# A two-layer trunk on one core: the causal mask of layer 1 as a VectorE addition in PSUM, the head's loads on two queues, and SP's loads in the order of the code

## The chip, the cores and the metric

The kernel runs on one core of one Trainium2 chip. The metric is device time in microseconds (us), the median of three executions; beside them one execution was profiled. The core's engines each work through a queue of their own, in order: TensorE (PE, with its weight loads as PEld), VectorE (DVE), ScalarE (ACT), GpSimd (POOL) and SyncE (SP), which only starts transfers here. ACT can start transfers too. Matmul results stand in PSUM, all else in SBUF.

## The reference

Two layers, each `x <- LayerNorm(ALPHA * x + mixer(x))`, on 256 tokens of 1024 values with 16 heads of 64. Layer 0 selects 64 keys for each query by an index score and runs softmax attention over them; layer 1 is stick-breaking attention, which the mask belongs to.

```python
def dsa_mixer(x, w_in, w_out, cos, sin):            # layer 0
    q, k, v, g, qi, wi, ki = split(x @ w_in)        # q, k, qi, ki get rope
    score = einsum('bqhs,bqh->bqs', relu(qi . ki * 64 ** -0.5), wi)
    _, idx = top_k(where(key_chunk <= q_chunk, score, -inf), 64)
    p = softmax(q . k[idx] * 64 ** -0.5)
    return (p @ v[idx] * silu(g)) @ w_out

def stick_breaking_mixer(x, w_in, w_out):           # layer 1
    q, k, v, g = split(x @ w_in, 4)
    z = einsum('bqhd,bshd->bhqs', q, k) * 64 ** -0.5
    before = pos[None, :] < pos[:, None]            # key strictly earlier than query
    log_one_minus = where(before, log_sigmoid(-z), 0.0)
    log_stick = cumsum(log_one_minus, axis=3, reverse=True) - log_one_minus
    a = where(before, exp(log_sigmoid(z) + log_stick), 0.0)
    return (a @ v * silu(g)) @ w_out
```

## The kernel before, in words

Numbers are kept to 32-bit accuracy by splitting each operand into a high part (written by ACT as a copy to `fp32r`) and a low part (DVE: source minus high), and by three matmuls for each product. `split` (L65 to L67) does it: `wh`, `wl` are the parts of a chunk of weights, `xT` those of the transposed input, `sh`, `sl` those of the stick logits.

**Weights.** They stream as 80 chunks of 128x1024 (512 KB) over SP's queue. `fetch` (L79) starts the load of a chunk into one of four `raw` buffers and splits it; `load_chunk` keeps two chunks ahead (`AHEAD`). A load can start only when its `raw` buffer has been split.

**Head.** `WARM` matmuls on zeros (L167) run on PE first. Eight loads `x_idx` (L172 to L179) bring, for each of the eight slices k of the model dimension, 256 columns of transposed x and 584 columns of index weights; the first slice comes in two loads, one on SP and one on ACT. Behind them come the first chunk, the constants `cs` (identity, triangle, causal mask, rope tables), and a copy `cr` of three of them by POOL. The index projections are the matmuls of L228; `rope` (L211 to L218, tiles `ra` and `rb`) rotates them, and PE transposes them to `qih`, `qil` (L249, L250) and `zh`, `zl` (padded keys).

**Layer 0.** `mix` runs the projections of half of q, k and v (`tok_part`, L113) turn by turn with `select` (index scores L136, top-64). Then a loop over pairs of heads runs key transposes, logits, softmax and values of successive pairs in one iteration, with the other projections, the gates (L145) and the output projection in between. At its fifth step (`s == 4`) the program text has the two loads of `x` and the two of `gb` (layer-norm scale and shift, 128x1024 each). `out_norm` is the output projection with the residual and layer norm.

**Layer 1.** Values and gates first, with the loads of layer 1's `gb` ahead of them. Then one loop over pairs j, with the stages of different pairs in one iteration: `queries1` (L158 is the copy `low`, L159 adds it in PSUM, `zh`/`zl` are the padded queries), `values1` every second pair, `keys1` (`kh`, `kl`), `logits1` of the pair before and `sticks1` of the one before that. `logits1` writes, for each of two key tiles t, three matmuls (L573 is the last) and the mask (L576) into a PSUM bank; then ACT takes abs, exp and ln (`ab`, L579 to L581), DVE max/add (L582), and the result is split to `sh`, `sl`. `sticks1` adds the triangle products of them (L595 to L597) into the same banks, and ACT takes the exponential `aw` (L602).

**Order.** A tile scheduler sets the order of each engine's queue before the run, by its own estimates and not strictly by the program text; `keep_in_program_order` pins an instruction to its place in the text. So a load can stand in SP's queue far ahead of where the text has it, or behind it.

Of the kernel before, what the change touches and what calls it, by code (L numbers as in the profile page):

```python
# [10 lines left out]
F32R = mybir.dt.float32r  # L11
AF = mybir.ActivationFunctionType
OP = mybir.AluOpType

P = 128
S = 256
D = 1024
KT = D // P
NT = S // P
# [13 lines left out]
IDX_W = IH * HD + HD + IH  # L33
# [4 lines left out]
C_ID, C_TRI, C_CAUS, C_ADM0, C_ADM1, C_COS, C_SIN = 0, 128, 256, 384, 512, 768, 896  # L38
# [4 lines left out]
def trunk(ctx: ExitStack, tc: tile.TileContext, x_rows, x_idx, w_all, consts, lnp, out):  # L43
    nc = tc.nc

    def pool(name, bufs, **kw):
        return ctx.enter_context(tc.tile_pool(name=name, bufs=bufs, **kw))
# [4 lines left out]
    cst = pool("cst", 1)  # L52
# [7 lines left out]
    def as32(t):  # L60
        return t.bitcast(F32)
# [1 line left out]
    nc.scalar.preload_act_table_set("exp_and_others")  # L63

    def split(h, lo, src):  # L65
        nc.scalar.activation(h, src, AF.Copy)  # L66
        nc.vector.tensor_sub(lo, src, as32(h))  # L67


    def feature_major(name):  # L70
        a = sb.tile([P, KT, 2, S], F32R, name=name, tag="aT")
        return a, a[:, :, 0], a[:, :, 1]

    _, xTh, xTl = feature_major("xT")

    ahead = []
    n_chunk = [0]

    def fetch():  # L79
        c = n_chunk[0]  # L80
        if c == w_all.shape[0]:
            return
        n_chunk[0] += 1
        raw = wraw.tile([P, CW], F32, name="raw", tag="raw")
        nc.sync.dma_start(raw, w_all[c])
        wh = wspl.tile([P, CW], F32R, name="wh", tag="wh")
        wl = wspl.tile([P, CW], F32R, name="wl", tag="wl")
        split(wh, wl, raw)
        ahead.append((wh, wl))
# [9 lines left out]
    def bank(p, w=512):  # L99
        return p.tile([P, 512], F32, name="bank", tag="bank")[:, :w]  # L100
# [15 lines left out]
    def tok_block(src):  # L116

        ps = [bank(pp) for _ in range(NT)]
        for c, wc in enumerate(load_block()):
            if c:  # L120
                yield
            tok_part(list(enumerate(ps)), src, wc, c)
        return ps

    def mix(*gens):

        live = list(gens)
        while live:
            for g in list(live):
                try:  # L130
                    next(g)
                except StopIteration:
                    live.remove(g)
# [36 lines left out]
    cuts = (slice(0, IDX_A), slice(IDX_A, IDX_W))  # L170
    idx_w = []
    for k in range(KT):  # L172
        raw = wraw.tile([P, CW], F32, name="raw", tag="raw")[:, :S + IDX_W]
        if k:
            nc.sync.dma_start(raw, x_idx[k])
        else:
            first = S + IDX_A
            nc.sync.dma_start(raw[:, :first], x_idx[k, :, :first])
            nc.scalar.dma_start(raw[:, first:], x_idx[k, :, first:])  # L179
        wh = wspl.tile([P, CW], F32R, name="wh", tag="wh")[:, :IDX_W]  # L180
        wl = wspl.tile([P, CW], F32R, name="wl", tag="wl")[:, :IDX_W]
        split(xTh[:, k], xTl[:, k], raw[:, :S])
        for c in cuts[:1 + (k == 0)] if k == 0 else (slice(0, IDX_W),):
            split(wh[:, c], wl[:, c], raw[:, S + c.start:S + c.stop])
        idx_w.append((wh, wl))

    fetch()
    cs = cst.tile([P, C_W], F32, name="cs")
    nc.sync.dma_start(cs, consts)
    ident = cs[:, C_ID:C_ID + P]  # L190
    adm = [cs[:, C_ADM0:C_ADM0 + P], cs[:, C_ADM1:C_ADM1 + S]]
    cos = cs[:, C_COS:C_COS + P].rearrange("p (t d) -> p t d", t=2)
    sin = cs[:, C_SIN:C_SIN + P].rearrange("p (t d) -> p t d", t=2)
    cr = cst.tile([P, 3, P], F32R, name="cr")
    nc.gpsimd.tensor_copy(cr, cs[:, :3 * P].rearrange("p (a b) -> p a b", a=3))
    identr, trir, causr = cr[:, 0, :], cr[:, 1, :], cr[:, 2, :]
    onesr = cst.tile([P, P], F32R, name="onesr")
    neg1 = cst.tile([P, P], F32, name="neg1")
    nc.gpsimd.memset(neg1, -1.0)
# [22 lines left out]
    for k in range(KT):  # L222
        w = idx_w[k]
        for xp, wp in ((0, 0), (1, 0), (0, 1)):
            xk = (xTh, xTl)[xp]
            for t in range(NT):
                for n in range(2):
                    nc.tensor.matmul(psi[t][n][:, :cuts[n].stop - cuts[n].start],  # L228
                                     xk[:, k, t * P:(t + 1) * P], w[wp][:, cuts[n]],
                                     start=k + xp + wp == 0, stop=k == 7 and wp == 1)  # L230
    for _ in range(AHEAD):
        fetch()
# [14 lines left out]
    def feat_split(h, lo, src, scale=None):  # L247
        if scale is None:
            nc.scalar.activation(h, src, AF.Copy)  # L249
            nc.vector.tensor_sub(lo, src, as32(h))  # L250
        else:
            nc.scalar.activation(h, src, AF.Copy, scale=scale)
            nc.vector.scalar_tensor_tensor(lo, src, scale, as32(h), op0=OP.mult, op1=OP.subtract)
# [15 lines left out]
    for j in range(2):  # L269
# [5 lines left out]
        pv = pt.rearrange("p (a s) -> p a s", a=2)  # L275
# [38 lines left out]
    def q_block(half):  # L314
        ps = yield from tok_block(xs)
        rr = []
        for t in range(NT):
            r = wk.tile([P, 8, HD], F32, name=f"rq{t}", tag=f"s{t}")
            rope(r, ps[t], 8, t)
            rr.append(r)  # L320
        for j in range(2):
            pt = bank(at)
            for a in range(2):
                for t in range(NT):
                    nc.tensor.transpose(pt[:, (2 * a + t) * P:(2 * a + t + 1) * P],
                                        rr[t][:, 4 * j + 2 * a:4 * j + 2 * a + 2, :], ident)
            for a in range(2):
                g = 4 * half + 2 * j + a
                feat_split(qh[g], ql[g], pt[:, a * S:(a + 1) * S], -SCALE)
        yield  # L330

    def k_block(half):
        ps = yield from tok_block(xs)
        for t in range(NT):
            rope(kr[t][:, 8 * half:8 * half + 8], ps[t], 8, t)
        yield
# [18 lines left out]
    def v_block(n):  # L355
        tiles = yield from tok_block(xs)
        for t, ps in enumerate(tiles):
            keep_v(ps, n, t)
        yield
# [92 lines left out]
    g_b = {}  # L452
# [44 lines left out]
    def load_gb(layer):  # L497
        for i in range(2):
            g_b[layer, i] = cst.tile([P, D], F32, name=f"gb{layer}{i}", tag=f"gb{i}")
            nc.sync.dma_start(g_b[layer, i], lnp[2 * layer + i:2 * layer + i + 1, :].to_broadcast([P, D]))  # L500

    def chain(*gens):
        for g in gens:
            yield from g

    def gates(src):
        for j in range(NPAIR):
            gate(j, src)
            yield

    x = [sb.tile([P, D], F32, name=f"x{t}", tag=f"x{t}") for t in range(NT)]
# [10 lines left out]

    mix(chain(q_block(0), k_block(0), v_block(0)), select())
    fill = chain(k_block(1), q_block(1), v_block(1), gates(xs), out_norm(0, x, turn))
    for s in range(NPAIR + 3):
        if s == 4:
            for t in range(NT):
                nc.sync.dma_start(x[t], x_rows[t * P:(t + 1) * P, :])
            load_gb(0)
        for c in "kfvFlft":  # L530
            if c == "f" or (c == "F" and s < 4):
                next(fill, None)
            elif c != "F":
                d, stage = {"k": (0, keys0), "l": (1, logits0), "t": (2, turn0), "v": (3, values0)}[c]
                if 0 <= s - d < NPAIR:
                    stage(s - d)
    for _ in fill:
        pass
    load_gb(1)


    ys = [(yTh[:, k], yTl[:, k]) for k in range(KT)]
# [21 lines left out]
    def logits1(j):  # L564
        z = zpad[j % 2]
        kh, kl = held.pop(j)
        pz, sp = [], []
        for t in range(NT):
            n = (NT - t) * P
            ks = slice(t * P, (t + 1) * P)  # L570
            pv = bank(at, 2 * n).rearrange("p (a q) -> p a q", a=2)
            qs = slice(t * P, S)
            nc.tensor.matmul(pv, kh[:, ks], z[0][:, :, qs], start=True, stop=False)  # L573
            nc.tensor.matmul(pv, kh[:, ks], z[1][:, :, qs], start=False, stop=False)
            nc.tensor.matmul(pv, kl[:, ks], z[0][:, :, qs], start=False, stop=False)
            nc.tensor.matmul(pv[:, :, :P], identr, causr[:, None, :].to_broadcast([P, 2, P]),  # L576
                             start=False, stop=True)
            a = wk.tile([P, 2, n], F32, name=f"ab{t}", tag=f"b{n}")
            nc.scalar.activation(a, pv, AF.Abs)  # L579
            nc.scalar.activation(a, a, AF.Exp, scale=-1.0)  # L580
            nc.scalar.activation(a, a, AF.Ln, bias=1.0)  # L581
            nc.vector.scalar_tensor_tensor(a, pv, 0.0, a, op0=OP.max, op1=OP.add)  # L582
            sh = wk.tile([P, 2, n], F32R, name=f"sh{t}", tag=("s0", "pT0")[t])
            sl = wk.tile([P, 2, n], F32R, name=f"sl{t}", tag=("s1", "pT1")[t])
            split(sh, sl, a)
            pz.append(pv)
            sp.append((sh, sl))
        held[j] = pz, sp
# [19 lines left out]
            weighted_v(*((jj, lambda i, aw=held[jj]: aw[0][:, i, :], lambda i, aw=held[jj]: aw[1][:, i, :])  # L608
                         for jj in (j - 1, j)))

    for _ in gates(ys):
        pass
    tc.keep_in_program_order(nc.scalar.preload_act_table_set("natural_log_exp_and_others"))
    def store(t, n):
        ns = slice(n * 512, (n + 1) * 512)
# [92 lines left out]
```

## Time and profile before

| | us |
|---|---|
| three runs, median | 315.13 |
| the three runs | 314.31, 315.13, 315.16 |
| profiled execution, its own time | 313.89 |
| its span in the trace | 312.1 |
| PE busy | 299.8 (96%) |
| DVE busy | 246.3 (79%) |
| ACT busy | 191.7 (61%) |
| POOL busy | 7.7 (2%) |

The profiled execution is one more run with its own time; the span is what its trace covers, and 1.79 us lie around it. Busy shares are means over the whole span: stages with different limits lie behind them.

### The profile page before, as it was taken

Reading aid. Unit: us, or ns where it says so; the run is one execution under the profiler, and the core shown is the slowest. Engines: PE = TensorE matmul, PEld = TensorE weight load, DVE = VectorE, ACT = ScalarE, POOL = GpSimd, SP = SyncE. Lnnn points to the kernel's source line nnn. Section 1 sums busy time; section 2 is a strip of 40 time slices with the busy share of each in tenths; the row PEclk is TensorE's granted clock in tenths of the full one; section 3 lists DMA queues with packets and bytes.
Section 4 is the critical chain, followed back from the end, with each engine's and each line's share of the span. In section 5 each row is a group of like instructions: output and inputs, shape, how many; then the busy total and the mean of one; then the engine's idle time right before and its main releaser. Section 6 shows DMA issues by size and latency. Waiting matters only on the chain.

```text
span 312.1 us, 4825 instructions
## 1 busy us (share of the span) xinstructions
PE 299.8 (96%) x1722; PEld 256.3 (82%) x1722; DVE 246.3 (79%) x538; ACT 191.7 (61%) x388; POOL 7.7 (2%) x16
## 2 busy tenths in 40 slices
PE   8998799998999999999999999999999999999990
PEld 5986688886888899988888888888888888887790
DVE  3777989998999999997589576776788887872375
ACT  5655445385346998875415377657799998975200
POOL 3010000000000000000010100000000000000011
PEclk9999799999999999999999999999999999999997
DMA  7898736586044846574424858866553253000003
GB/s 255 270 328 284 274 111 202 186 280 209 4 131 137 268 138 187 186 234 140 133 67 127 275 161 295 287 197 198 167 163 100 69 159 100 2 0 2 0 13 121
DMA packets 14423, 50.40 MB, mean 161 GB/s; under 512 B 1600, under 2 KB 1728, under 8 KB 14400
## 3 DMA queue, kind: packets, MB, share of 16 engines
q1 hardware_dynamic: 14256, 49.97, 49.3%
q8 instruction: 13, 0.21, 0.3%
q10 hardware_dynamic: 144, 0.14, 0.1%
q14 instruction: 10, 0.08, 0.1%
HBM read 49.05 MB, written 1.05 MB: 161 GB/s over the span
## 4 chain that ended last, share of the span: by engine, by line
PE 78%; DVE 10%; DMA 6%; issue 3%; ACT 2%; DVEq 0%; SPq 0%; ACTq 0%
PE bank L113 32%; PE bank L153 14%; PE bank L145 7%; PE bank L155 7%; DMA raw<-w_all 4%; DVE wl L67 4%; PE bank L368 3%; DMA raw<-x_idx 2%; PE bank L596 1%; PE bank L136 1%; PE bank L369 1%; DVE sc L293 1%; ACT wh L66 1%; DVE sc L300 1%; PE bank L138 1%
## 5 line engine op out<-in xcount | busy, mean ns | idle before, releaser
L67 DVE TENSOR_TENSOR wl<-raw,wh 128x1024 fp32r<-128x1024 f32 (+2 forms) x89 | 103.5, 1165 | 23.1 <-ACT wh L66 22.4
L66 ACT ACTIVATE wh<-raw 128x1024 fp32r<-128x1024 f32 (+2 forms) x89 | 90.0, 1016 | 50.2 <-DMA raw<-w_all 25.6
L113 PE MATMUL bank<-wh,xT 128*128 128x512 f32 x192 | 50.8, 400 | 1.2 <-DVE rb L216 1.2
L153 PE MATMUL bank<-yT,wh 128*128 128x512 f32 x192 | 48.3, 394 | 0.0
L113 PEld LDWEIGHTS bank<-wh,xT 128*128 128x128 f32 x192 | 35.9, 191 | 8.7 <-issue 1.6
L153 PEld LDWEIGHTS bank<-yT,wh 128*128 128x128 f32 x192 | 34.5, 189 | 6.9 <-issue 0.3
L155 PEld LDWEIGHTS bank<-yT,wl 128*128 128x128 f32 x192 | 26.2, 190 | 1.9
L113 PE MATMUL bank<-wl,xT 128*128 128x512 f32 x96 | 27.6, 396 | 0.0
L155 PE MATMUL bank<-yT,wl 128*128 128x256 f32 x192 | 26.8, 282 | 0.0
L113 PEld LDWEIGHTS bank<-wl,xT 128*128 128x128 f32 x96 | 18.4, 192 | 3.7
L113 PE MATMUL bank<-wh,ol 128*128 128x512 f32 (+1 forms) x80 | 20.5, 350 | 0.0
L113 PE MATMUL bank<-wh,oh 128*128 128x512 f32 (+1 forms) x80 | 20.4, 354 | 0.0
L113 PE MATMUL bank<-wl,oh 128*128 128x512 f32 (+1 forms) x80 | 20.2, 348 | 0.0
L113 PE MATMUL bank<-wh,yT 128*128 128x512 f32 x64 | 17.4, 391 | 0.0
L145 PE MATMUL bank<-xT,wh 128*128 128x256 f32 x128 | 16.9, 285 | 0.0
L425 ACT ACTIVATE p<-ml,mx 128x128 f32<-128x128 f32 (+1 forms) x32 | 14.3, 447 | 3.7 <-DVE mx L420 3.4
L145 PEld LDWEIGHTS bank<-xT,wh 128*128 128x128 f32 x128 | 16.1, 190 | 0.4
L113 PEld LDWEIGHTS bank<-wh,ol 128*128 128x128 f32 x80 | 14.1, 189 | 2.1 <-issue 0.2
L113 PEld LDWEIGHTS bank<-wl,oh 128*128 128x128 f32 x80 | 14.1, 189 | 1.9
L113 PEld LDWEIGHTS bank<-wh,oh 128*128 128x128 f32 x80 | 13.6, 189 | 2.2 <-issue 0.5
L113 PEld LDWEIGHTS bank<-wh,yT 128*128 128x128 f32 x64 | 12.0, 188 | 2.4
L582 DVE SCALAR_TENSOR_TENSOR ab<-bank,ab 128x512 f32<-128x512 f32 (+1 forms) x16 | 8.5, 555 | 6.3 <-ACT ab L581 5.9
(140 smaller groups left out, 507.3 us busy)
## 6 DMA issues: line engine op xcount, KB each, us to landing
raw<-w_all SPq DMA_DIRECT2D x80, 512.0 KB, 4.3
raw<-x_idx SPq DMA_DIRECT2D x7, 420.0 KB, 4.1
gb<-lnp SPq DMA_DIRECT2D x4, 512.0 KB, 6.9
x<-x_rows SPq DMA_DIRECT2D x2, 512.0 KB, 6.5
y<-x SPq DMA_DIRECT2D x4, 256.0 KB, 2.0
cs<-consts SPq DMA_DIRECT2D x1, 512.0 KB, 6.8
raw<-x_idx SPq DMA_DIRECT2D x1, 288.0 KB, 2.9
raw<-x_idx ACTq DMA_DIRECT2D x1, 132.0 KB, 3.1
```

What stands on the lines that cost most here:

```text
L66: nc.scalar.activation(h, src, AF.Copy)
L67: nc.vector.tensor_sub(lo, src, as32(h))
L113: nc.tensor.matmul(ps, src[kk][xp][:, t * P:(t + 1) * P], wc[wp][:, k, :], start=kk == 0 and xp + wp == 0, stop=kk == 7 and wp == 1)
L136: nc.tensor.matmul(ps, sh, mh, start=first, stop=False)
L138: nc.tensor.matmul(ps, sl, mh, start=False, stop=last)
L145: nc.tensor.matmul(ps, w[wp][:, k, :], src[k][xp], start=k + xp + wp == 0, stop=k == 7 and wp == 1)
L153: nc.tensor.matmul(ps, wh[:, k, :], yT[:, k], start=k == 0, stop=k == 7)
L155: nc.tensor.matmul(ps[:, :S], wl[:, k, :], yTh[:, k], start=False, stop=k == 7, skip_group_check=True)
L293: nc.vector.scalar_tensor_tensor(sc, rel[:, a, :], wi[t][:, h:h + 1], prev, op0=OP.mult, op1=OP.add)
L368: nc.tensor.matmul(po[rs, n * S:(n + 1) * S], vt[0][:, hs], p0(i), start=True, stop=False)
L425: nc.scalar.activation(p[:, i, :], m[:, i, :], AF.Exp, bias=mx[:, c], scale=-1.0, accum_out=sm[:, c])
L582: nc.vector.scalar_tensor_tensor(a, pv, 0.0, a, op0=OP.max, op1=OP.add)
```

## The change

It has three parts. (1) The causal mask of layer 1 is added by DVE to the logits where they stand in PSUM, and no longer by a matmul of the identity with the mask; of the three constants that POOL copied only the triangle is still needed. (2) The first slice of the head comes in three loads (x on SP, 320 columns of weights on ACT, 264 on SP), slices 1 and 3 are loaded by ACT's queue, the x part of the first slice is split by DVE alone, and ACT's two copies for it are pinned in program order. (3) All of SP's loads are pinned in program order, the x rows and layer 0's `gb` come one at each step from the fifth on, and layer 1's `gb` are loaded in its gates, the first behind two of them.

```diff
+    def load(dst, src):
+        tc.keep_in_program_order(nc.sync.dma_start(dst, src))
...
-        nc.sync.dma_start(raw, w_all[c])
+        load(raw, w_all[c])
...
         if k:
-            nc.sync.dma_start(raw, x_idx[k])
+            (nc.scalar.dma_start if k in (1, 3) else load)(raw, x_idx[k])
         else:
             first = S + IDX_A
-            nc.sync.dma_start(raw[:, :first], x_idx[k, :, :first])
-            nc.scalar.dma_start(raw[:, first:], x_idx[k, :, first:])
+            load(raw[:, :S], x_idx[k, :, :S])
+            nc.scalar.dma_start(raw[:, S:first], x_idx[k, :, S:first])
+            load(raw[:, first:], x_idx[k, :, first:])
...
-        split(xTh[:, k], xTl[:, k], raw[:, :S])
...
+        if k:
+            split(xTh[:, k], xTl[:, k], raw[:, :S])
+        else:
+            nc.vector.tensor_copy(xTh[:, k], raw[:, :S])
+            nc.vector.tensor_sub(xTl[:, k], raw[:, :S], as32(xTh[:, k]))
+        for c in cuts if k == 0 else (slice(0, IDX_W),):
+            copy = split(wh[:, c], wl[:, c], raw[:, S + c.start:S + c.stop])
+            if k == 0:
+                tc.keep_in_program_order(copy)
...
-    cr = cst.tile([P, 3, P], F32R, name="cr")
-    nc.gpsimd.tensor_copy(cr, cs[:, :3 * P].rearrange("p (a b) -> p a b", a=3))
-    identr, trir, causr = cr[:, 0, :], cr[:, 1, :], cr[:, 2, :]
+    caus = cs[:, C_CAUS:C_CAUS + P]
+    trir = cst.tile([P, P], F32R, name="trir")
+    nc.gpsimd.tensor_copy(trir, cs[:, C_TRI:C_TRI + P])
...
-            nc.sync.dma_start(g_b[layer, i], lnp[2 * layer + i:2 * layer + i + 1, :].to_broadcast([P, D]))
+            load(g_b[layer, i], lnp[2 * layer + i:2 * layer + i + 1, :].to_broadcast([P, D]))
+            yield
...
+    def rows():
+        for t in range(NT):
+            load(x[t], x_rows[t * P:(t + 1) * P, :])
+            yield
+
+    extra = chain(rows(), load_gb(0))
     for s in range(NPAIR + 3):
-        if s == 4:
-            for t in range(NT):
-                nc.sync.dma_start(x[t], x_rows[t * P:(t + 1) * P, :])
-            load_gb(0)
+        if s >= 4:
+            next(extra, None)
...
-    load_gb(1)
...
-            nc.tensor.matmul(pv, kl[:, ks], z[0][:, :, qs], start=False, stop=False)
-            nc.tensor.matmul(pv[:, :, :P], identr, causr[:, None, :].to_broadcast([P, 2, P]),
-                             start=False, stop=True)
+            nc.tensor.matmul(pv, kl[:, ks], z[0][:, :, qs], start=False, stop=True)
+            nc.vector.tensor_add(pv[:, :, :P], pv[:, :, :P], caus[:, None, :].to_broadcast([P, 2, P]))
...
-    for _ in gates(ys):
-        pass
+    mix(gates(ys), chain((None for _ in range(2)), load_gb(1)))
```

On SP's queue this is the stretch of the kernel before behind the constants, with the loads of weights (`raw`), layer-norm rows (`gb`, named by their number) and x rows:

```order
L85 DMA raw<-w_all 128x1024 x6
L500 DMA gb_1165<-lnp 128x1024
L500 DMA gb_1167<-lnp 128x1024
L85 DMA raw<-w_all 128x1024
L528 DMA x_373<-x_rows 128x1024
L85 DMA raw<-w_all 128x1024 x2
L528 DMA x_374<-x_rows 128x1024
L85 DMA raw<-w_all 128x1024 x42
L500 DMA gb_2015<-lnp 128x1024
L500 DMA gb_2017<-lnp 128x1024
```

And this is the same stretch of the changed kernel:

```order
L79 DMA raw<-w_all 128x1024 x25
L79 DMA x_374<-x_rows 128x1024
L79 DMA raw<-w_all 128x1024 x2
L79 DMA x_375<-x_rows 128x1024
L79 DMA raw<-w_all 128x1024 x2
L79 DMA gb_1424<-lnp 128x1024
L79 DMA raw<-w_all 128x1024 x2
L79 DMA gb_1565<-lnp 128x1024
L79 DMA raw<-w_all 128x1024 x21
L79 DMA gb_2258<-lnp 128x1024
L79 DMA raw<-w_all 128x1024
L79 DMA gb_2290<-lnp 128x1024
```

The four loads that stood behind the sixth to ninth chunk after the constants now stand behind the 25th to 31st, one at a time, and layer 1's two have a chunk between them.

On ACT's queue this is one iteration of layer 1's loop before, for the pair whose stick logits are `ab_3059` and `ab_3073` (pair 5, counted from 0); `aw` are the exponentials of the pair ahead of it, `sh` the high parts:

```order
L579 ACTIVATE ab_3059<-bank 128x512
L579 ACTIVATE ab_3073<-bank 128x256
L580 ACTIVATE ab_3059<-ab_3059 128x512
L580 ACTIVATE ab_3073<-ab_3073 128x256
L249 ACTIVATE kh<-bank 128x256
L581 ACTIVATE ab_3059<-ab_3059 128x512
L581 ACTIVATE ab_3073<-ab_3073 128x256
L602 ACTIVATE aw_3088<-bank 128x512
L602 ACTIVATE aw_3090<-bank 128x256
L66 ACTIVATE sh_3064<-ab_3059 128x512
L66 ACTIVATE sh_3078<-ab_3073 128x256
L158 ACTIVATE low<-bank 128x256
```

And this is the same pair in the changed kernel, where the numbers are one higher:

```order
L617 ACTIVATE aw_3091<-bank 128x256
L617 ACTIVATE aw_3089<-bank 128x512
L261 ACTIVATE kh<-bank 128x256
L594 ACTIVATE ab_3060<-bank 128x512
L594 ACTIVATE ab_3074<-bank 128x256
L595 ACTIVATE ab_3060<-ab_3060 128x512
L595 ACTIVATE ab_3074<-ab_3074 128x256
L596 ACTIVATE ab_3060<-ab_3060 128x512
L596 ACTIVATE ab_3074<-ab_3074 128x256
L163 ACTIVATE low<-bank 128x256
L66 ACTIVATE wh<-raw 128x1024
L66 ACTIVATE sh_3065<-ab_3060 128x512
```

The exponentials `aw` have moved from behind the logarithms to ahead of the abs, and a copy `low` and a weight copy `wh` now stand between the logarithms and `sh`.

On DVE's queue this is the same pair in the changed kernel, from the addition of `low` for its iteration to the low parts `sl`; before, the rows from `kl` on were `kl`, the two max/add, the two `sl`, the addition of `low` and `wl`:

```order
L164 TENSOR_TENSOR bank<-bank,low 128x256
L592 TENSOR_TENSOR bank<-bank,cs 128x2x128
L592 TENSOR_TENSOR bank<-bank,cs 128x256
L67 TENSOR_TENSOR wl<-raw,wh 128x1024
L262 TENSOR_TENSOR kl<-bank,kh 128x256
L597 SCALAR_TENSOR_TENSOR ab_3060<-bank,ab_3060 128x512
L597 SCALAR_TENSOR_TENSOR ab_3074<-bank,ab_3074 128x256
L164 TENSOR_TENSOR bank<-bank,low 128x256
L67 TENSOR_TENSOR wl<-raw,wh 128x1024
L67 TENSOR_TENSOR sl_3066<-ab_3060,sh_3065 128x512
L67 TENSOR_TENSOR sl_3080<-ab_3074,sh_3079 128x256
```

The two masks (L592) are new, one for each key tile, and the addition of the next `low` and a weight split `wl` have moved ahead of `sl`.

## Rows read from the trace of the kernel before

**Rows 1.** The page: span, and busy time of each engine.

```profile
span 312.1 us, 4825 instructions
PE 299.8 (96%) x1722; PEld 256.3 (82%) x1722; DVE 246.3 (79%) x538; ACT 191.7 (61%) x388; POOL 7.7 (2%) x16
```

**Rows 2.** Windows by stage: us, busy, PE clock, DMA share, GB/s.

```profile
4.50:18.80 14.30, 14.30 (x97) 14.25 (x97) 9.42 (x18) 8.35 (x16) 0.37 (x1) 1.00 0.90 307
...
33.00:75.00 42.00, 42.00 (x190) 34.77 (x191) 40.52 (x92) 22.27 (x32) 0.00 (x0) 0.96 0.62 208
75.00:174.00 99.00, 97.71 (x628) 85.73 (x627) 89.00 (x238) 61.42 (x146) 1.91 (x2) 1.00 0.47 148
174.00:222.00 48.00, 48.00 (x258) 41.35 (x256) 31.98 (x43) 30.28 (x47) 0.00 (x0) 1.00 0.72 231
222.00:284.00 62.00, 61.99 (x378) 53.48 (x378) 47.83 (x89) 54.74 (x124) 0.00 (x0) 1.00 0.28 86
```

**Rows 3.** Timeline, end of the head: start, us, engine, what [idle before <-releaser].

```profile
18.28 1.23 DVE L67 TENSOR_TENSOR wl<-raw,wh 128x1024 fp32r<-128x1024 f32 x1 [2.11 <-ACT wh L66]
...
18.86 2.00 PE L113 MATMUL bank<-wh,xT 128*128 128x512 f32 x8
...
19.43 0.48 DVE L215 TENSOR_TENSOR ra<-bank,cs 128x320 f32<-128x320 f32 x1
```

**Rows 4.** Timeline of SP's queue: chunk, gb pair, a later chunk.

```profile
23.67 0.33 SPq L85 DMA_DIRECT2D raw<-w_all  x1
24.05 0.90 SPq L500 DMA_DIRECT2D gb<-lnp  x2
...
84.79 0.33 SPq L85 DMA_DIRECT2D raw<-w_all  x1
```

**Rows 5.** Timeline, 29 to 89 us: the waits and what ended them.

```profile
29.75 1.06 ACT L66 ACTIVATE wh<-raw 128x1024 fp32r<-128x1024 f32 x1 [1.58 <-DMA raw<-w_all]
...
31.32 0.69 DVE L250 TENSOR_TENSOR qil<-bank,qih 128x512 fp32r<-128x512 f32 x1 [2.42 <-ACT qih L249]
...
32.85 0.36 PE L136 MATMUL bank<-zh,qih 128*128 128x256 f32 x1 [2.10 <-issue]
...
43.28 0.76 DVE L253 SCALAR_TENSOR_TENSOR ql<-bank,qh 128x256 fp32r<-128x256 f32 x2 [1.07 <-ACT qh L252]
...
75.85 0.43 DVE L250 TENSOR_TENSOR zl<-bank,zh 64x256 fp32r<-64x256 f32 x1 [0.91 <-ACT zh L249]
...
77.70 1.17 PE L113 MATMUL bank<-wh,xT 128*128 128x512 f32 x4 [1.16 <-DVE rb L216]
...
88.39 1.06 ACT L66 ACTIVATE wh<-raw 128x1024 fp32r<-128x1024 f32 x1 [1.47 <-DMA raw<-w_all]
```

**Rows 6.** Windows of 4 us behind L136's wait (columns as in rows 2).

```profile
32.00:36.00 4.00, 3.15 (x15) 2.89 (x16) 3.91 (x7) 2.10 (x4) 0.00 (x0) 0.80 0.64 247
36.00:40.00 4.00, 4.00 (x17) 3.22 (x17) 4.00 (x12) 1.33 (x2) 0.00 (x0) 0.78 0.75 268
```

**Rows 7.** Groups by line, 222 to 312 us: count, busy, mean ns, idle before.

```profile
L159 DVE TENSOR_TENSOR bank<-bank,low 128x256 f32<-128x256 f32 x14 | 6.0, 427 | 0.1
```

**Rows 8.** Timeline, one pair of layer 1's loop, up to the sticks' use.

```profile
265.29 0.28 PE L576 MATMUL bank<-cr 128*128 128x256 f32 x1
...
265.41 0.28 PE L573 MATMUL bank<-zh,kh 128*128 128x256 f32 x1
...
265.82 0.87 ACT L579 ACTIVATE ab<-bank 128x512 f32<-128x512 f32 x2
...
269.92 1.03 DVE L67 TENSOR_TENSOR sl<-ab,sh 128x512 fp32r<-128x512 f32 x2 [0.56 <-ACT sh L66]
...
274.16 0.28 PE L595 MATMUL bank<-sl,cr 128*128 128x256 f32 x1
```

**Rows 9.** Timeline, the last pair.

```profile
282.82 0.87 ACT L579 ACTIVATE ab<-bank 128x512 f32<-128x512 f32 x2 [2.53 <-PE bank L576]
...
286.68 0.19 PEld L596 LDWEIGHTS bank<-sh,cr 128*128 128x128 f32 x1 [0.15 <-ACT sh L66]
```

More of the change, by code (lines that the diff above doesn't have):

```diff
@@ L65, in split @@
     def split(h, lo, src):
-        nc.scalar.activation(h, src, AF.Copy)
+        copy = nc.scalar.activation(h, src, AF.Copy)
         nc.vector.tensor_sub(lo, src, as32(h))
+        return copy
     def feature_major(name):
@@ L174, in trunk @@
         if k:
-            nc.sync.dma_start(raw, x_idx[k])
+            (nc.scalar.dma_start if k in (1, 3) else load)(raw, x_idx[k])
         else:
             first = S + IDX_A
-            nc.sync.dma_start(raw[:, :first], x_idx[k, :, :first])
-            nc.scalar.dma_start(raw[:, first:], x_idx[k, :, first:])
+            load(raw[:, :S], x_idx[k, :, :S])
+            nc.scalar.dma_start(raw[:, S:first], x_idx[k, :, S:first])
+            load(raw[:, first:], x_idx[k, :, first:])
         wh = wspl.tile([P, CW], F32R, name="wh", tag="wh")[:, :IDX_W]
         wl = wspl.tile([P, CW], F32R, name="wl", tag="wl")[:, :IDX_W]
-        split(xTh[:, k], xTl[:, k], raw[:, :S])
-        for c in cuts[:1 + (k == 0)] if k == 0 else (slice(0, IDX_W),):
-            split(wh[:, c], wl[:, c], raw[:, S + c.start:S + c.stop])
+        if k:
[7 more added lines that the diff above has]
+                tc.keep_in_program_order(copy)
         idx_w.append((wh, wl))
@@ L188, in trunk @@
     cs = cst.tile([P, C_W], F32, name="cs")
-    nc.sync.dma_start(cs, consts)
+    load(cs, consts)
     ident = cs[:, C_ID:C_ID + P]
```

## The prediction

> **What bounds the kernel now.** I read the page first: PE is busy 96% of the span and DVE 79% [rows 1]. A share is an average, so next come busy times in windows that follow the program's stages [rows 2]: the reader is to see where PE falls short of its window, and which other engine is full beside it. In 33 to 75 us PE is busy 42.00 of 42.00, but DVE 40.52 too: index scores, selection, rope and weight splits run beside the first projections, and that DVE work must be done before PE may go on. From 75 to 284 PE is full (97.71 of 99, 48.00 of 48, 61.99 of 62), so there only work taken off PE, or a wait put on it, moves the end. ACT is the second load of the last stage, 54.74 of 62 us.
>
> Then I looked, in the timeline, for the few places where something waits.
> - Head: PE is full from 4.50 to 18.80 [rows 2]; behind that, DVE gets its first chunk split at 18.28 after 2.11 us idle and reaches the first rope product `ra` at 19.43, although the index matmuls are done when L113 starts at 18.86 [rows 3].
> - 24 to 45 us: SP issues a chunk at 23.67 and the two layer-norm rows `gb` (1 MB) at 24.05, behind it at once [rows 4]. That chunk's split starts at 29.75, 6.1 us after its issue; ACT has waited 1.58 for it. A chunk alone (issued 84.79, split at 88.39 after a wait of ACT for it) takes 3.6 [rows 4, 5]. ACT works in order, so `qih` comes behind the late split, DVE waits 2.42 for it, and PE 2.10 before L136 [rows 5]. In 32 to 40 PE's granted clock is 0.80 and 0.78 over 4 us each [rows 6]: after that idle time part of the stretch ran at the half level (1.2 GHz). At 43.28 DVE waits 1.07 more, for an ACT copy behind PE's transposes. Then DVE is nearly full until `rb` releases PE at 77.70, where PE has idled 1.16 [rows 5].
>
> **The change part by part.**
>
> *Head.* The first three matmul operands in pieces can't move PE before 4.50: it is on its warm-up products until then, and from there full to 18.80 [rows 2]. What can move is the first weight chunk, with two loads fewer on SP's queue ahead of it, and so DVE's 19.43. The matmuls it needs end about 18.86, so the bounds are 0 and 19.43 − 18.86 = 0.57; the shown waits stand on the DMA side, so I take 0.4. The x split moved from ACT to DVE (one cast) and the small `trir` copy lie beside PE's full stretch: nothing; uncovered, one 128x256 DVE operation is 0.43 [rows 7].
>
> The Trainium skill ("DMA: Bandwidth & Descriptors", section "Issuing engines are not separate DMA queues") says that loads started from another engine run on the same 16 DMA engines and save only the time of issuing. SP's issues here are about 0.4 apart [rows 4], so two loads moved to ACT would be worth about 0.8 of issuing, and no bytes; no run here shows more.
>
> *x and gb out of 24 to 36 us.* Before, the rows `gb`, `gb`, `x`, `x` (2 MB) stand among the chunks that q and selection need; now they come behind the 25th to 31st chunk after the constants, one at a time. The split at 29.75 could then start when ACT is free, 29.75 − 1.58 = 28.17; with 3.6 from issue to split it would be ready at 27.3, with 4.7 (some load still beside it) at 28.4. So 0.8 to 1.58; I take 1.5, as the quiet price gives room. The 1.07 at 43.28 was a PE transposition running late behind the 2.10 wait and the half clock: both go, so I take it whole (bounds 0, 1.07). Sum at `rb`: 1.5 + 1.07 = **2.57**. DVE's 0.91 at 75.85, a wait for another split's chain, stays [rows 5]; if it went too, another 0.91. PE alone would gain more: 1.58, and the half clock's (0.20 + 0.22) × 4 = 1.68 [rows 6]. But DVE sets `rb`, so PE's wait at 77.70 grows to 1.16 + 1.58 + 1.68 − 2.57 = 1.85.
>
> *Where they go instead.* These chunks belong to 75 to 174 us (DMA share 0.47), the new place of gb(1) to 174 to 222 (0.72) [rows 2]: PE is full in both with chunks loaded two ahead, which is the cover. Nothing; without that cover each of the six costs up to one landing's excess, 6.1 − 3.6 = 2.5.
>
> *The mask.* PE loses 16 matmuls L576. By their starts one takes 0.12 (265.29, then the next product at 265.41) [rows 8]; the record's 0.28 is pipelined. 16 × 0.12 = 1.92. DVE gets 16 additions in PSUM, nearest to L159 (PSUM and SBUF in, PSUM out, same 256 columns), 427 ns [rows 7]: 16 × 0.43 = 6.8, beside 47.83 of 62 busy. They fit, if they are not late. The waits they add: DVE's add waits for PE's three logit products, and queued behind it are `kl`, a weight split and the max/add; ACT's abs waits for the add. The order of ACT also changes: the exponentials `aw` of the previous pair come ahead of abs, and they wait for stick products that PE does behind the logits. Those are six, of 256 or 512 columns: 2 × (0.12 + 0.24 + 0.12) = 0.96 by the 0.12 above, and `aw` then takes about the 0.87 of the abs pair, which has the same shapes [rows 8]; with a hop between them the whole abs-exp-ln-split chain starts about 2 us later (an estimate). What waits for the chain's end is PE's L595 of the next iteration: for the pair at 265.82 the low part ends at 269.92 + 1.03 = 270.95, used at 274.16 [rows 8], a slack of 3.2. Two us plus two adds (0.86) is 2.9: just inside. In the pairs (3 and 5 of 0 to 7) where DVE's order puts `wl`, 1.23 [rows 3], ahead of `sl`, it is 4.1, and 0.9 outside, unless abs starts sooner than I think. I count nothing for it here and make it a rival.
>
> The last pair has no work behind it: ACT waits 2.53 for L576 at 282.82, and the sticks wait for its chain (286.68) [rows 9]. There the add is on the path, 0.43 − 0.12 = 0.31, and its two matmuls win nothing. Net: 14 × 0.12 − 0.31 = **1.37**; bounds: 1.92 if the tail finds cover, −0.6 if the two late pairs lose 0.9 each.
>
> **Sum.** 0.4 + 2.57 + 1.37 = 4.34. The profiled execution takes 313.89 (span 312.1 [rows 1] and 1.79 around it), so such a one would take 309.55. It lies 1.24 under the median of the three runs, 315.13; the mean of all four is 314.62, and against that the forecast is 314.62 − 4.34 = **310.3**. Times here tell 0.3% (0.95 us) from no change.
>
> **Rivals.**
> - *The late chunk isn't due to gb.* The transfers may be slow at that time whatever stands behind the chunk. For it: the DMA share is still 0.64 and 0.75 in 32 to 40 [rows 6], when gb's loads should be over, and `gb` was issued behind this chunk, not ahead of it. Against: a chunk with nothing behind it takes 3.6. Then only the head and the mask count: 314.62 − 1.77 = 312.85.
> - *The clock at 77.70.* A wait of 2.10 was followed by the half level, one of 1.16 was not [rows 5, 6]; 1.85 lies between. If it falls, 1.68 is lost: 312.0. The Trainium skill ("TensorE: Matmul & The Clock Gate", section "HAM oscillation — how this bites in real kernels") tells that idle gaps between bursts of matmuls bring the clock back to half rate; by that rule a longer wait there costs more than its own length, and the fall behind L136's wait agrees with it.
> - *Only the joint stage fails.* The two late pairs cost 1.8 and eat the 1.37: 314.62 − 2.97 + 0.4 = 312.1.
> - *The other side: slower.* All eight pairs' chains come late, since mask, `aw` and abs now follow each other PE-DVE-ACT in each iteration. It decides from 4.34 / 8 = 0.55 us of stall per pair; with the 0.9 of the late pairs in each of eight, 7.2: 314.62 − 4.34 + 7.2 = 317.5. For it: ACT is at 54.74 of 62. Against: 3.2 of slack in an ordinary pair, where I find 2.9 used.
> - *The change doesn't do what it says:* the new order of SP's and ACT's queues shows it does; no chance of its own.
>
> **Chances.** Forecast 0.46 (its own range 309.2 to 311.4: sums of 3.2 to 5.4, where 5.4 is the upper bounds 0.57, 2.65 and 1.92 with some of the 0.91); late chunk not due to gb 0.14; clock 0.14; joint stage fails 0.16; slower 0.10. The low end goes to 308.2, from the upper bounds with the full 0.91 (6.05) against 314.3, the fastest of the three; the high end, 313.3, takes in three rivals with part of a second miss. Slower by over 0.3%: 0.09, the last rival. Within 0.3%: 0.11, where two rivals meet (312.85 + 1.77 is no change). Faster: 0.80.
>
> **What would show it.** Right: the split that stood at 29.75 starts about 28.2 and `qil` waits under 1; the clock in 32 to 40 is 1.00; PE starts on `rb` near 75; no L576, 16 additions of about 0.43 on DVE; from there to the end of the joint stage 1.4 less; ACT's wait for the last pair's abs longer by 0.3. Wrong: PE waits for `sl` in each iteration of the joint stage; a clock under 1.00 behind 75 us; a new DMA wait of ACT near the 25th to 31st chunk.

## The result, and the profile after

| | kernel before | changed kernel | ratio, 95% interval |
|---|---|---|---|
| first comparison, median (runs) | 315.14 (4) | 310.97 (4) | 0.9873 [0.983, 0.9917] |
| the same two kernels later, beside the last experiments | 312.97 (29) | 310.79 (6) | 0.9933 [0.9908, 0.9957] |

The change makes the kernel faster: by 4.2 us in the first comparison, by 2.2 in the second. The changed kernel's time is nearly the same in both; it is the kernel before that moved. Its 29 runs lie between 311.23 and 315.25 us, and the first four (314.31 to 316.29) lay in the upper part of that or above it. The two intervals meet at 0.991 to 0.992; the larger sample is the better measure, a gain of about 2.2 us.

The page of the changed kernel (this execution took 310.63 us), the lines that answer to [rows 1]:

```profile
span 308.7 us, 4810 instructions
PE 297.0 (96%) x1706; PEld 252.9 (82%) x1706; DVE 250.3 (81%) x555; ACT 191.0 (62%) x387; POOL 7.5 (2%) x16
```

DVE has 4.0 us more to do, PE 2.8 less in its records, and PE is still busy 96%. The windows of the changed kernel that answer to [rows 2, 6]:

```profile
33.00:75.00 42.00, 41.04 (x191) 33.24 (x189) 40.40 (x94) 22.43 (x34) 0.00 (x0) 1.00 0.62 200
...
174.00:222.00 48.00, 47.77 (x254) 40.98 (x253) 31.37 (x43) 30.65 (x48) 0.00 (x0) 1.00 0.67 223
222.00:284.00 62.00, 62.00 (x367) 52.51 (x365) 52.82 (x106) 55.73 (x129) 0.00 (x0) 1.00 0.27 83
...
32.00:36.00 4.00, 4.00 (x23) 3.30 (x22) 3.91 (x8) 1.86 (x4) 0.00 (x0) 1.00 0.56 145
36.00:40.00 4.00, 4.00 (x24) 3.34 (x23) 3.73 (x12) 2.52 (x4) 0.00 (x0) 1.00 0.30 117
```

PE's clock is 1.00 from 32 to 40 us, where it was 0.80 and 0.78. In the joint stage DVE takes 52.82 of 62 us, 5.0 more, and PE is busy in all 62. The timeline of the changed kernel at the places of [rows 3, 5], and one new wait of PE in the gates, with the split of a late chunk ahead of it:

```profile
19.73 0.48 DVE L227 TENSOR_TENSOR ra<-bank,cs 128x320 f32<-128x320 f32 x1
...
28.48 1.06 ACT L66 ACTIVATE wh<-raw 128x1024 fp32r<-128x1024 f32 x1 [0.72 <-DVE wl L67]
...
31.59 0.59 PE L141 MATMUL bank<-zh,qih 128*128 128x256 f32 x3 [0.56 <-issue]
...
75.60 1.16 PE L118 MATMUL bank<-wh,xT 128*128 128x512 f32 x4 [1.40 <-DVE rb L228]
...
199.90 1.06 ACT L66 ACTIVATE wh<-raw 128x1024 fp32r<-128x1024 f32 x1 [1.96 <-DMA raw<-w_all]
...
204.07 2.11 PE L158 MATMUL bank<-yT,wh 128*128 128x512 f32 x8 [0.23 <-DVE sg L405]
```

The split that waited for its transfer at 29.75 now waits for DVE at 28.48, PE idles 0.56 before the first index score and not 2.10, and `rb` releases PE 2.10 earlier. `qil` waits 0.89. `ra` is not earlier but 0.30 later.

Then the joint stage. These two lines are the first product of `logits1` in the kernel before (a second profile of it, run e12 below) and in the changed kernel; behind the durations stand the starts of the first and the last of the sixteen (L573, now L589, is the first of the three products for a key tile; the last is L575, now L591):

```profile
L573 PE MATMUL bank<-zh,kh x16: 282/336/396, 222.0 to 281.9; 128*128 128x512 f32 x8, 128*128 128x256 f32 x8
```

```profile
L589 PE MATMUL bank<-zh,kh x16: 278/334/396, 221.2 to 279.1; 128*128 128x512 f32 x8, 128*128 128x256 f32 x8
```

59.9 us have become 57.9. That difference of stretches is the cleanest number of this study: in five profiles with the mask on PE (before, e12, e2, e7, e8) the stretch is 59.8 to 59.9, in nine with it on DVE 57.9 to 58.0. From the last of these starts to the end of the span it is 29.4 to 29.5 in the five, and 29.5 to 29.6 in the nine. Against e12, which like the changed kernel ran with its clock at 1.00 in 32 to 40, the gain of 2.6 us of span (311.3 to 308.7) falls so: 1.3 up to `rb` (76.91 to 75.60), then 0.5 lost up to the first logits (222.0 to 221.2 is 0.8), 2.0 won in the joint stage, 0.2 lost behind it.

### The profile page after: what moved, and what is told of

Read it like the earlier page. It is cut to its first block, busy times and chain, and to the rows that moved or that the text cites. A ratio compares the mean times of both kernels' runs of the same rounds, so it can differ in the third digit from the quotient of the medians.

```text
span 308.7 us, 4810 instructions
## 1 busy us (share of the span) xinstructions
PE 297.0 (96%) x1706; PEld 252.9 (82%) x1706; DVE 250.3 (81%) x555; ACT 191.0 (62%) x387; POOL 7.5 (2%) x16
## 4 chain that ended last, share of the span: by engine, by line
PE 76%; DVE 10%; DMA 9%; ACT 2%; issue 2%; DVEq 0%; SPq 0%; ACTq 0%
PE bank L118 30%; PE bank L158 15%; PE bank L150 7%; PE bank L160 7%; DMA raw<-w_all 7%; DVE wl L67 4%; PE bank L380 3%; DMA raw<-x_idx 2%; ACT wh L66 2%; PE bank L611 1%; PE bank L381 1%; PE bank L141 1%; DVE sc L312 1%; PE bank L590 1%; PE bank L589 1%
## 5 line engine op out<-in xcount | busy, mean ns | idle before, releaser
L118 PEld LDWEIGHTS bank<-wh,xT 128*128 128x128 f32 x192 | 35.2, 188 | 9.5 <-issue 2.0
```

The lines of the kernel that those rows point to most:

```text
L118: nc.tensor.matmul(ps, src[kk][xp][:, t * P:(t + 1) * P], wc[wp][:, k, :], start=kk == 0 and xp + wp == 0, stop=kk == 7 and wp == 1)
```

## The experiments

Each was timed in 6 to 12 runs beside 29 to 35 of the kernel before, on one chip for each group: e1, e2, e4, e6; then e3, e5, e7, e8; then e9 to e12. In every group the kernel before had a median of 312.96 to 312.98 us. The profiled execution is one of the runs and need not be a typical one: in e4 it is the second shortest of twelve, in e7 and e11 the longest.

**The three parts, one at a time.**

Mask alone (e1): the kernel before with this edit, and `trir` in place of `cr`.

```diff
-            nc.tensor.matmul(pv, kl[:, ks], z[0][:, :, qs], start=False, stop=False)
-            nc.tensor.matmul(pv[:, :, :P], identr, causr[:, None, :].to_broadcast([P, 2, P]),
-                             start=False, stop=True)
+            nc.tensor.matmul(pv, kl[:, ks], z[0][:, :, qs], start=False, stop=True)
+            nc.vector.tensor_add(pv[:, :, :P], pv[:, :, :P], caus[:, None, :].to_broadcast([P, 2, P]))
```

> The kernel before with the mask alone moved to DVE. By the theory that PE's sixteen mask products were the cost and DVE's additions are covered, the first logits of layer 1 stand where they stood (222.8 us) and the last pair's logits come 1.7 to 1.8 us earlier than 281.83; the time falls by 1.4 to 1.8 us, to about 313.5. By the rival that the joint stage gained from the earlier chunks and not from the mask, nothing moves: 315.1.

311.63 us, ratio 0.9962 [0.9934, 0.9989]: 1.2 us by the ratio. Logits from 221.5 to 279.5 us, 58.0: the joint stage has its whole gain without the other parts. Their places were expected as in the first profile of before; this execution's `rb` released PE at 76.30 and not at 77.70, so only stretches can be compared.

Moves alone (e8): the kernel before with all of SP's loads pinned, x and `gb` late as in the change; head and mask as before.

```diff
-        nc.sync.dma_start(raw, w_all[c])
+        load(raw, w_all[c])
...
-        if s == 4:
-            for t in range(NT):
-                nc.sync.dma_start(x[t], x_rows[t * P:(t + 1) * P, :])
-            load_gb(0)
+        if s >= 4:
+            next(extra, None)
```

> The kernel before with the pinned loads and the later x and gb alone: old head, mask on PE. If the three parts add, this is the moves' part: rb releases PE 2.1 to 2.6 us earlier than 77.70, half a us is lost in the gates, and the time is 312.6 to 313.4. If the moves pay only together with the mask or the new head, 315.1.

312.34, ratio 0.9971 [0.9938, 1.0004]: 0.9 us, with an interval that touches no change. PE idles 0.34 before the first score and `rb` releases it at 75.75. The wait is gone as forecast, and less time came of it. The half us expected to be lost in the gates is not lost here.

Head alone (e7): the kernel before with the new head, nothing pinned on SP. (e3, below, has the head's part without the other order of the queue that came of this.)

```diff
+            nc.sync.dma_start(raw[:, :S], x_idx[k, :, :S])
+            nc.scalar.dma_start(raw[:, S:first], x_idx[k, :, S:first])
+            nc.sync.dma_start(raw[:, first:], x_idx[k, :, first:])
...
+            (nc.scalar.dma_start if k in (1, 3) else nc.sync.dma_start)(raw, x_idx[k])
```

> The kernel before with the new head alone, SP's loads not pinned. The scheduler then puts the constants and the two gb loads ahead of index slices on SP's queue (1.5 MB ahead of five of eight slices). By the theory that the head is bound by its transfers this makes PE wait before 20 us, by 2 to 5 us: 317 to 320. By the rival that the warm-up and the index products cover any order, 315.1.

313.00, ratio 1.0003 [0.9975, 1.0031]. SP's queue came out with constants and `gb` among the index slices:

```
L179 DMA raw<-x_idx 128x256
L181 DMA raw<-x_idx 128x264
L197 DMA cs<-consts 128x1024
L176 DMA raw<-x_idx 128x840
L508 DMA gb_1166<-lnp 128x1024
L508 DMA gb_1168<-lnp 128x1024
L176 DMA raw<-x_idx 128x840 x4
```

PE does wait for it in the index products, as this timeline of e7 shows, 2.0 us in two waits:

```profile
10.53 1.34 PE L236 MATMUL bank<-wh,xT 128*128 128x320 f32 x8 [1.21 <-ACT wh L66]
...
14.84 1.36 PE L236 MATMUL bank<-wh,xT 128*128 128x320 f32 x8 [0.78 <-ACT wh L66]
```

The loss was expected, but not that the time would stay the same. With `gb` gone from 24 us PE idles only 0.63 before the first score, and starts on `rb` at 77.73. That is near the 77.70 of before, but the half clock is in that row. Beside the profiles of the old loads without it (76.30 in e1, 76.91 in e12) it is 0.8 to 1.4 later, and beside those without the late split (75.33 to 75.76, below) 2.0 to 2.4. So the head's 2.0 us do arrive at `rb`, and the late split, which this run does not have, is what they are set off against; one run does not tell the two apart.

By time, the parts taken alone bring 1.2 (mask), 0.9 (moves) and nothing (head): 2.1 together, where the whole brings 2.2. Each of these is known to about 1 us.

**One part taken out of the changed kernel.**

Mask back on PE (e2), the edit of e1 reversed.

> The changed kernel with the mask back on PE. If the mask's part adds to the others, it takes 1.4 to 1.8 us more than the changed kernel, about 312.6; if the rest of the change already made the joint stage shorter, it stays at 311.0.

312.31, ratio 0.998 [0.9954, 1.0006] beside 0.9933 for the changed kernel: 1.5 us, as expected, though the two intervals just meet. Logits 221.1 to 280.9: 59.8.

Old head (e3): the head's two loads of the first slice and SP's other seven as before, pinned.

> The changed kernel with the head of before (first slice in two loads, all others on SP, splits by ACT and DVE as before), loads pinned. The prediction gave the head 0.4 us of gain: then this takes 311.4 and the first ra comes 0.4 later than 19.73. By what the changed kernel's trace shows (ra 0.30 later than before) it takes 310.7 and ra stands at 19.4.

310.9, ratio 0.9941 [0.9907, 0.9975] beside 0.9933: no difference that these runs can tell. `ra` stands at 18.49, but it is at 19.60 in a second profile of the changed kernel and at 18.32 to 20.00 in e4, e5, e6 and e11, which have the new head too: it varies by over 1 us between executions, and one pair of profiles could not have priced the head.

`gb` of layer 1 out of the gates (e6):

```diff
-    mix(gates(ys), chain((None for _ in range(2)), load_gb(1)))
+    for _ in gates(ys):
+        pass
...
+    extra = load_gb(1)
     for s in range(NPAIR + 3):
+        if s >= 3:
+            next(extra, None)
```

> The changed kernel with layer 1's two gb loads moved out of its gates into the loop over pairs. By the theory that these loads make a chunk of the gates late and so cost PE's wait at 204.07 (0.4 us with what follows), the wait is gone and the time falls by 0.4 to 0.5, to 310.5. By the rival that the wait comes from the order of DVE and ACT in the gates, wait and time stay.

310.48, ratio 0.9921 [0.9893, 0.995]. PE waits nowhere in the gates, and from their first product (187.2) to the first logits (221.0) it takes 33.8 us where the changed kernel takes 34.2. The stretch agrees with the theory; the time can't be told from the changed kernel's 0.9933.

**Which transfer made the chunk late?**

Both `gb` early again (e4), x late. The lines stand in `fetch` of the changed kernel:

```diff
         load(raw, w_all[c])
+        if c == 6:
+            for _ in load_gb(0, (0, 1)):
+                pass
```

> The changed kernel with layer 0's two gb loads put back on SP's queue right behind the sixth chunk after the constants, x left late. By the theory that gb's 1 MB delays that chunk, its split comes over 1 us later, part of the stretch from 32 to 40 us runs at the half clock again, rb releases PE 1.5 to 2.4 us later than 75.60, and the time is 312.5 to 313.4. By the rival that the chunk was late for another reason, 311.0 and rb at 75.6.

311.33, ratio 0.9953 [0.9921, 0.9985]. This is the run that my theory lost. SP's and ACT's timelines of e4, and then of e12 (the kernel before):

```profile
23.43 0.33 SPq L79 DMA_DIRECT2D raw<-w_all  x1
23.81 0.90 SPq L79 DMA_DIRECT2D gb<-lnp  x2
...
28.25 1.06 ACT L66 ACTIVATE wh<-raw 128x1024 fp32r<-128x1024 f32 x1 [0.75 <-DVE wl L67]
...
75.40 1.16 PE L129 MATMUL bank<-wh,xT 128*128 128x512 f32 x4 [1.41 <-DVE rb L239]
```

```profile
23.61 0.33 SPq L85 DMA_DIRECT2D raw<-w_all  x1
23.99 0.90 SPq L500 DMA_DIRECT2D gb<-lnp  x2
...
29.63 1.06 ACT L66 ACTIVATE wh<-raw 128x1024 fp32r<-128x1024 f32 x1 [2.13 <-DMA raw<-w_all]
...
32.73 0.59 PE L136 MATMUL bank<-zh,qih 128*128 128x256 f32 x3 [2.04 <-issue]
...
76.91 1.17 PE L113 MATMUL bank<-wh,xT 128*128 128x512 f32 x4 [1.55 <-DVE rb L216]
```

The queue of e4 has the chunk and both `gb` loads at the same distance as that of the kernel before, and here the split comes 4.82 us after the issue, held by DVE and not by a transfer. In the kernel before it comes 6.02 after it (e12), 6.06 (e1, with the same loads: 23.17 and 29.23) and 6.08 in its first profile, each time held by the transfer. In the profiles with x and `gb` both late it is 4.35 to 4.78, and 4.35 to 4.63 where the transfer ended the wait. In the three with the late split x can hardly have begun the delay: its first load was issued at 28.60, 28.55 (e12) and 28.10 (e1), behind the place where such a chunk would have landed (issue plus 4.63: 28.30, 28.24 and 27.80).

One `gb` early (e5): the same lines with `(0,)` in place of `(0, 1)`.

> As the run with both gb loads behind the sixth chunk, but with one of them (512 KB); the other stays late. If the bytes behind the chunk delay it, the cost is about half of that of two: rb 0.7 to 1.3 us later than 75.60, 311.9. If only the place in SP's queue matters, it is as large as with two; if neither, 311.0.

310.86, ratio 0.9928 [0.9898, 0.9958]: no cost. Its profile has `rb` at 77.45, but all of it runs late from the first chunk on (`ra` 20.00), and PE idles only 0.72 before the first score.

x early (e11): the two x loads behind the seventh and ninth chunk, `gb` late.

```diff
         load(raw, w_all[c])
+        if c in (7, 9):
+            x_row(c // 8)
```

> The changed kernel with the two x loads put back behind the seventh and ninth chunk, gb left late. With gb alone early the first index scores did not come later. If x is what delays the chunks, PE idles about 2 us before the first index score again and rb releases PE 0.7 us or more later than 75.60: 311.7. If neither does it alone, 311.0 and an idle time under 0.8: then it takes both, or the delay is one of single executions.

310.94, ratio 0.9936 [0.9908, 0.9964]: no cost either, and 0.67 of idling before the first score at 31.14. Its `rb` came late for another reason, at 77.31. This is e11's timeline (ACT, DVE, PE), and the two windows behind it:

```profile
73.96 1.06 ACT L66 ACTIVATE wh<-raw 128x1024 fp32r<-128x1024 f32 x1 [2.61 <-DMA raw<-w_all]
...
75.46 0.43 DVE L270 TENSOR_TENSOR zl<-bank,zh 64x256 fp32r<-64x256 f32 x1 [2.19 <-ACT zh L269]
...
77.31 2.04 PE L126 MATMUL bank<-wh,xT 128*128 128x512 f32 x4 [2.60 <-DVE rb L236]
```

```profile
74.00:78.00 4.00, 1.40 (x6) 0.86 (x5) 2.47 (x8) 3.49 (x4) 0.00 (x0) 0.87 0.21 86
78.00:82.00 4.00, 4.00 (x14) 3.15 (x13) 4.00 (x13) 0.00 (x0) 0.00 (x0) 0.70 0.00 2
```

A chunk landed late, ACT in its order did the copy `zh` behind it, DVE waited 2.19 for that, `rb` came late, PE idled 2.60, and the clock fell: 0.87 and 0.70, a mixture of the full and the half level (0.50 in each us from 77 to 80). The rival on the clock at `rb` is real; here it came with a wait of 2.60, where the 1.40 of the changed kernel had no fall behind it.

**The kernels themselves, again.**

Changed kernel (e9), kernel before (e12), and a version meant to be best (e10: the changed kernel with the edits of e3 and e6).

> The changed kernel itself, again, in many runs beside many of the kernel before. In these the kernel before has taken 313.1 on the mean, not 315.1, with 1 to 1.5 us between single runs. If the four runs of the first comparison flattered the change, it takes about 311.0, a gain of 2 and not 4. If they did not, about 309.

310.79, ratio 0.9933: the smaller gain of the two that were expected. `rb` at 75.65 as in the first profile; but PE's wait in the gates is now 0.87, behind a split that waited 2.56 for its chunk at 200.67, and the first logits stand at 222.0.

> The kernel before itself, with a second profile. If the half clock behind 34 us belongs to the kernel, the stretch from 32 to 40 us shows 0.8 again and rb stands at 77.7. If it is a matter of the single execution, the clock may be 1.00 there with the same 2 us of waiting, rb near 76.3, as in the run with the mask alone, and the profiled time nearer 312.5.

313.47, ratio 0.9993 [0.9961, 1.0026], as it should be for the same kernel. Its windows that answer to [rows 6]:

```profile
32.00:36.00 4.00, 3.27 (x19) 2.88 (x20) 3.91 (x6) 2.10 (x4) 0.00 (x0) 1.00 0.65 214
36.00:40.00 4.00, 4.00 (x21) 3.07 (x20) 4.00 (x12) 1.81 (x4) 0.00 (x0) 1.00 0.84 265
```

The wait of PE is there (2.04), the fall of the clock is not. So the late chunk belongs to the kernel before, in three profiles of three, and the half clock to single executions, one of these three.

> The changed kernel with the old head (pinned) and layer 1's gb loads in the loop over pairs. If both parts add, ra stands near 18.8 in place of 19.73, nothing waits in the gates, and it takes 0.4 to 0.8 less than the changed kernel: 310.3. If ra only varies from execution to execution, the old head brings nothing and only the 0.4 of the gates is left: 310.6.

311.02, ratio 0.9931 [0.991, 0.9951]: not faster than the changed kernel's 0.9933. `ra` stands at 18.69 and nothing waits in the gates, but PE starts on `rb` at 75.76, where it starts in all profiles with x and `gb` late (75.33 to 75.76). In these seven profiles `ra` lies between 18.49 and 19.73: a us won in the head does not show at that point.

## Why the prediction was right, step by step, and where a step was not

The time, 310.97 (and 310.79 later), is 0.7 from the forecast of 310.3, in the narrow range too, and the direction was right. That it was hit so closely is luck in part, for two errors stood against each other: the gain was forecast at 4.34 and is about 2.2, and the time from which it was taken, 314.62 (a mean of four), is above the 313.0 that the larger sample shows. The signs it named came in the changed kernel's trace (split at 28.48, `qil` waiting 0.89, clock 1.00, `rb` at 75.60), but part of what they were compared with was one execution's.

- **Mask, forecast 1.37: right in mechanism, a little small.** 14 × 0.12 − 0.31 counted both masks of the last pair as winning nothing, but the first of them stood ahead of the pair's second tile on PE. The stretch between first and last logits holds 15 masks, 1.8, and is 1.8 to 2.0 shorter; behind it 0.1 to 0.2 is lost, about the forecast's 0.31 less the 0.12 of the last mask. Net 1.7 to 1.8 by the traces; by the times 1.2 (e1) and 1.5 (e2 against the changed kernel). The lower bound given as −0.6 comes out as 1.37 − 1.8 = −0.43.
- **Price of the addition: right.** 422 ns against 427, as this line of the changed kernel's groups shows, and hidden, since PE is busy in all of the stage:

```profile
L592 DVE TENSOR_TENSOR bank<-bank,cs 128x256 f32<-128x256 f32 x16 | 6.4, 422 | 1.1 <-PE bank L591 1.1
```

- **The rival "only the joint stage fails": wrong, by a hair.** This is pair 5 in the changed kernel, at the places of [rows 8]: the last logits, abs, the low parts, and the product that uses them. Ahead of them stands the last logits product of the same pair in the kernel before.

```profile
265.64 0.28 PE L575 MATMUL bank<-zh,kl 128*128 128x256 f32 x1
```

```profile
262.55 0.28 PE L591 MATMUL bank<-zh,kl 128*128 128x256 f32 x1
...
264.57 0.88 ACT L594 ACTIVATE ab<-bank 128x512 f32<-128x512 f32 x2
...
269.49 1.02 DVE L67 TENSOR_TENSOR sl<-ab,sh 128x512 fp32r<-128x512 f32 x2
...
270.74 0.28 PE L610 MATMUL bank<-sl,trir 128*128 128x256 f32 x1
```

  Abs starts 2.02 behind the last logits (before: 0.18), about 2 later, as estimated; the low parts end at 270.51, and PE wants them at 270.74. The slack of 3.2 has shrunk to 0.2: 3.0 of it is used, where 2.9 was forecast for an ordinary pair and 4.1 for this one. The 3.0 are 1.84 of later start, 0.81 more from abs to the end of `sl`, and 0.33 by which PE comes to the sticks sooner. Of the 0.81 the copies in front of `sh` make 0.2 and `wl` in front of `sl` 0.6, not 1.23; the additions, which the sum of 4.1 put on top of the later start, are inside it. PE waits for `sl` in no pair.
- **Tail: right.** ACT's wait for the last abs went from 2.53 to 2.02 instead of growing, because its queue came to it later, but the chain is longer by the add: abs starts 0.90 behind the first tile's last logits product (278.90), where it was 0.54 (282.28), so 0.36 more for a forecast of 0.31.

```profile
279.80 0.87 ACT L594 ACTIVATE ab<-bank 128x512 f32<-128x512 f32 x2 [2.02 <-DVE bank L592]
...
283.83 0.19 PEld L611 LDWEIGHTS bank<-sh,trir 128*128 128x128 f32 x1 [0.39 <-ACT sh L66]
```

- **Head, forecast 0.4: wrong, nothing.** The row of `ra` at 19.43, taken for a mark of the kernel, was one draw from 18.3 to 20.0, and what is won there does not reach `rb` (e10). The Trainium skill ("DMA: Bandwidth & Descriptors", section "Issuing engines are not separate DMA queues") has loads started from another engine run on the same 16 DMA engines. e3 agrees with it: two slices put back from ACT's queue to SP's cost no time that these runs can tell (0.9941 and 0.9933).
- **x and `gb` late, forecast 2.57: the step that was mis-sized.** It took the late split, the half clock and the 1.07 at 43.28 as properties of the kernel. Only the first is: the wait of 2.0 to 2.1 shows in all three profiles of the old loads and in none of the eleven others. Between executions without the half clock the moves bring 0.5 to 1.6 at `rb` (76.30 and 76.91 against 75.33 to 75.76), and 0.9 by time (e8). The half clock, and with it the 1.07 wait, was that one execution's: from the first score to `rb` it takes 44.85 us, and 44.18 and 43.97 in the other two of the old loads, so it cost 0.7 to 0.9. (The 0.8 given as the lower bound for the late split does not follow from its rows: 29.75 − 28.4 is 1.35.)
- **Its cause, "`gb` behind the chunk": not shown.** Neither `gb` alone (e4) nor x alone (e11) brings the late split back, in one profile each. The profile of e4 is of one of its shortest executions, so others may have been late. x was issued too late to begin the delay. The old head with `gb` early in the pinned order was not run, nor both early, so what makes the chunk late stays open.
- **Cover for the loads in their new place: half right.** x and layer 0's `gb` cost nothing where they went (no wait of PE of 0.1 us or more between 76 and 187 in the changed kernel). Layer 1's `gb` in the gates do make a chunk late: in all eight profiles that have them there, ACT waits 1.27 to 2.56 for the chunk that it splits 11.5 to 13.6 us behind the first gate product, and in the six others it waits for no transfer at that place. PE's own slack takes most of it. The stretch from the first gate product to the first logits is 33.7 to 33.8 in ten of the fourteen profiles, also with those loads in the gates and ACT waiting up to 2.01 (e3); it is 34.2, 34.1 and 34.9 in the three where ACT waits 1.96, 2.22 and 2.56 (changed kernel, e2, e9). The fourth, e7, has the loads ahead of the gates and 34.2 beside a wait of ACT of 1.33 for an earlier chunk (split at 194.90). So the cover was just large enough, not ample; by time the 0.4 could not be told (e6, e10).
- **The clock at `rb`.** PE's wait there was forecast to grow to 1.85; it is 1.40 and 1.25, with the clock at 1.00. At this place the longest without a fall is 1.77 (e5), the one with a fall 2.60 (e11).

## What to carry to other kernels

A row of one trace is one draw: before a wait, or the clock behind it, is counted as a gain, it should be seen in a second profile of the same kernel, and stretches between two fixed products compare better than places from the start. Where one engine is full from end to end, an operation moved off it pays its start-to-start time for each instance, as long as the longer chain on the others ends before its next use; here 0.2 us of 3.2 was left, so the next such move would not be free. Work won ahead of another engine's full stretch can be lost there: `ra` moved by 1.2 us between profiles here and `rb` by 0.4.

## What the runs showed of the hardware that was not expected

- Two executions of the kernel before and one of e1, which has the same loads, idled PE for 2.0 to 2.1 us at the same place, and the clock fell behind it in one. The Trainium skill ("TensorE: Matmul & The Clock Gate", section "HAM oscillation — how this bites in real kernels") has idle gaps bring the half rate back; these rows agree that they can (2.10 and 2.60) and show that a gap of this size need not (2.04 and 2.08).
- Single executions of the kernel before differ by up to 4 us (311.23 to 315.25 in the 29 runs beside e9 to e12). The four shortest have mean clocks of 0.992 to 0.996, the seven longest 0.988 to 0.995: a lower clock goes with a part of it, and what makes the rest was not found.
